# Grouped instance norm: the stores move to SP's queue, the loads to ScalarE's

## The chip, the cores and the metric

One Trainium2 chip; the program runs on one core. The time is the device time of one execution in microseconds, the median of several runs. A profile is one more execution, recorded by the hardware profiler. The engines of a core run side by side, each through its own queue of instructions in order: TensorE (PE), VectorE (DVE), ScalarE (ACT), GpSimd (POOL) and SyncE (SP). A transfer between memory and the on-chip buffer (a DMA) is issued by an instruction in the queue of SP, ScalarE or GpSimd and then carried out by the core's 16 DMA engines. An instruction waits at the head of its queue until the semaphores that it names have been raised, and all that stands behind it waits too.

## The reference

Each of 512 channels (4 images, 8 groups, 16 channels each) of 256 x 256 float32 values is normalized by its own mean and variance and scaled by its gamma:

```python
mu = x.mean(axis=(3, 4), keepdims=True)
var = ((x - mu) ** 2).mean(axis=(3, 4), keepdims=True)
x_norm = (x - mu) / np.sqrt(var + 1e-5)
out = x_norm * gamma[None, :, :, None, None]
```

Input and output have 134.22 MB each.

## The kernel before

A channel's 65,536 values are laid over S = 8 partitions, 8,192 to a partition, so 16 channels fill the 128 partitions. Such a piece is a unit: 128 x 8192 float32, 4,194,304 bytes, 32 KB to a partition. There are U = 32 units, and one loop over u (line 105) handles them. Six slots in the on-chip buffer (`slots`, AHEAD = 6) hold units: unit u lies in slot u % 6 from its load to the landing of its store, and is normalized in place. In the profile the slots appear as `xt`.

Ahead of the loop, GpSimd issues a small store into the output (`touch`, line 54, 16 x 128 values) and the load of gamma (line 55). The loads of units 0 to 5 are issued at line 57: units 1 and 3 by ScalarE, units 0, 2, 4 and 5 by SP. A loop of 60 `nop` calls for VectorE follows (lines 59 and 60). Then come constants: `navg`, a 128 x 128 matrix that adds up the 8 partitions of a channel and divides by minus the count; a first square root on ScalarE (line 78), which brings the table load with it; gamma spread over the partitions by VectorE and eight small matmuls (lines 83 to 94).

For a unit, in this order:

- line 107, VectorE: the sum over each partition, into `st`. It waits for the unit's load.
- line 108, ScalarE: the square with the sum of squares, into `st`. It waits for the same load. Its elementwise result goes to `junk`.
- line 116, TensorE: matmul of `navg` with `st`. It gives every partition minus the mean and minus the mean square (`ps`).
- line 117, VectorE: minus the variance (`nvar`).
- line 121, ScalarE: the standard deviation (`std`), called the root below.
- lines 125 and 127, VectorE: its reciprocal, times gamma (`scale`).
- line 130, VectorE: (value minus mean) times scale, in place in the slot.
- line 134, ScalarE's queue: the store of the unit, which waits for line 130.
- line 136, SP's queue: the load of unit u + 6 (through `load`, line 48), which waits until store u has landed, since it writes into the same slot.

The order is the program's own (`manual_schedule`): within an engine's queue the instructions stand as the loop writes them. So ScalarE's queue holds, for each unit, square, root, store; SP's queue holds loads alone; a load that waits on SP holds up only later loads, and a store that waits on ScalarE holds up the next unit's square.

Of the kernel before, what the change touches and what calls it, by code (L numbers as in the profile page):

```python
# [1 line left out]

# [4 lines left out]

F32 = mybir.dt.float32
U8 = mybir.dt.uint8
ALU = mybir.AluOpType  # L10
ACTF = mybir.ActivationFunctionType
AX = mybir.AxisListType


@with_exitstack
def kernel(
    ctx: ExitStack,
    tc: tile.TileContext,
    x: bass.AP,
    gamma: bass.AP,  # L20
    out: bass.AP,
):
    nc = tc.nc
    B, G, C, H, W = x.shape
    P = nc.NUM_PARTITIONS
    HW = H * W
    n_ch = B * G * C
    S = 8
    K = P // S
    F = HW // S  # L30
    U = n_ch // K
    NG = (G * C) // K
    AHEAD = 6
    assert HW % S == 0 and (G * C) % K == 0

    xv = x.rearrange("b g c h w -> (b g c h w)").rearrange("(u p f) -> u p f", p=P, f=F)
    ov = out.rearrange("b g c h w -> (b g c h w)").rearrange("(u p f) -> u p f", p=P, f=F)
    gv = gamma.rearrange("g c -> (g c)")

    data = ctx.enter_context(tc.tile_pool(name="data", bufs=1))  # L40
    singles = ctx.enter_context(tc.tile_pool(name="singles", bufs=1))
    psum = ctx.enter_context(tc.tile_pool(name="psum", bufs=4, space=bass.MemoryType.PSUM))
    ctx.enter_context(tc.manual_schedule())

    slots = [data.tile([P, F], F32, name=f"xt{i}") for i in range(AHEAD)]

    def load(u, queue):
        queue.dma_start(out=slots[u % AHEAD][:], in_=xv[u])  # L48


    g_row = singles.tile([1, G * C], F32, name="g_row")
    touch = singles.tile([16, 128], F32, name="touch")
    nc.vector.memset(touch[:], 0.0)  # L53
    nc.gpsimd.dma_start(out=ov[0][0::S, 0:128], in_=touch[:])  # L54
    nc.gpsimd.dma_start(out=g_row[:], in_=gv[None, :])  # L55
    for u in range(AHEAD):
        load(u, nc.scalar if u in (1, 3) else nc.sync)

    for _ in range(60):
        nc.vector.nop()  # L60

    eps_t = singles.tile([P, 1], F32, name="eps_t")
    nc.gpsimd.memset(eps_t[:], 1e-5)
    one = singles.tile([1, 1], F32, name="one")
    nc.gpsimd.memset(one[:], 1.0)
    navg = singles.tile([P, K, S], F32, name="navg")
    nc.gpsimd.memset(navg[:], -1.0 / HW)  # L67
    nc.gpsimd.affine_select(  # L68
        out=navg[:], in_=navg[:], pattern=[[-S, K], [0, S]], compare_op=ALU.is_ge,
        fill=0.0, base=0, channel_multiplier=1,  # L70
    )
    nc.gpsimd.affine_select(  # L72
        out=navg[:], in_=navg[:], pattern=[[S, K], [0, S]], compare_op=ALU.is_ge,
        fill=0.0, base=S - 1, channel_multiplier=-1,
    )
    navg_w = navg[:].rearrange("p k s -> p (k s)")
    root_eps = singles.tile([P, 1], F32, name="root_eps")
    nc.scalar.activation(out=root_eps[:], in_=eps_t[:], func=ACTF.Sqrt)  # L78
    g_rep = singles.tile([1, NG, K, S], F32, name="g_rep")
    g_ps = psum.tile([P, NG], F32, name="g_ps", bufs=1)  # L80
    g_col = singles.tile([P, NG], F32, name="g_col")

    nc.vector.tensor_copy(  # L83
        out=g_rep[:],
        in_=g_row[:].rearrange("o (n k) -> o n k", n=NG).unsqueeze(3).to_broadcast([1, NG, K, S]),
    )
    for n in range(NG):
        nc.tensor.matmul(  # L88
            out=g_ps[:, n : n + 1],
            lhsT=g_rep[:, n].rearrange("o k s -> o (k s)"),  # L90
            rhs=one[:],
            start=True, stop=True,
        )
    nc.vector.tensor_copy(out=g_col[:], in_=g_ps[:])  # L94

    junk = singles.tile([P, F], U8, name="junk")

    st = singles.tile([P, U, 2], F32, name="st")
    nvar = singles.tile([P, U], F32, name="nvar")
    std = singles.tile([P, U], F32, name="std")  # L100
    rstd = singles.tile([P, U], F32, name="rstd")
    scale = singles.tile([P, U], F32, name="scale")

    squares = []
    for u in range(U):
        t = slots[u % AHEAD]
        nc.vector.reduce_sum(out=st[:, u, 0:1], in_=t[:], axis=AX.X)  # L107
        square = nc.scalar.activation(  # L108
            out=junk[:], in_=t[:], func=ACTF.Square, accum_out=st[:, u, 1:2],
        )  # L110
        if u:

            tc.declare_no_dep(square.ins, squares[-1].ins, reason="junk, ordered by the root between")
        squares.append(square)
        ps = psum.tile([P, 2], F32, name="ps")
        nc.tensor.matmul(out=ps[:], lhsT=navg_w, rhs=st[:, u], start=True, stop=True)  # L116
        nc.vector.tensor_scalar(  # L117
            out=nvar[:, u : u + 1], in0=ps[:, 0:1], scalar1=ps[:, 0:1],
            scalar2=ps[:, 1:2], op0=ALU.mult, op1=ALU.add,
        )  # L120
        nc.scalar.activation(  # L121
            out=std[:, u : u + 1], in_=nvar[:, u : u + 1], func=ACTF.Sqrt,
            bias=eps_t[:], scale=-1.0,
        )
        nc.vector.reciprocal(out=rstd[:, u : u + 1], in_=std[:, u : u + 1])  # L125
        g = u % NG
        nc.vector.tensor_mul(  # L127
            out=scale[:, u : u + 1], in0=rstd[:, u : u + 1], in1=g_col[:, g : g + 1],
        )
        nc.vector.tensor_scalar(  # L130
            out=t[:], in0=t[:], scalar1=ps[:, 0:1], scalar2=scale[:, u : u + 1],
            op0=ALU.add, op1=ALU.mult,
        )
        nc.scalar.dma_start(out=ov[u], in_=t[:])
        if u + AHEAD < U:
            load(u + AHEAD, nc.sync)


# [1 line left out]
_INS = ['x', 'gamma']  # L140
_OUTS = [((4, 8, 16, 256, 256), 'float32')]


# [23 lines left out]
```

## Time and profile before

| | |
|---|---|
| median of 3 runs | 627.01 us (626.89 to 627.01) |
| span of the profiled execution | 625.8 us |
| moved | 268.46 MB, mean 429 GB/s over the span |
| VectorE busy | 443.4 us (71%) |
| ScalarE busy | 238.8 us (38%) |
| TensorE busy | 21.4 us (3%) |
| line 107, reduction | 32 x 8684 ns |
| line 108, square | 32 x 7030 ns |
| line 130, normalize | 32 x 4550 ns |
| store, issue to landing | 62.5 us (median) |
| load by SP, issue to landing | 38.5 us (median) |

The profile has several views. The page's slices cut the span into 40 equal parts and give the busy share of each engine in tenths and what the DMA engines moved. The table by stretch gives the same for chosen intervals; its columns are the interval, its length, the busy time of each engine with the number of instructions, the granted clock, the DMA share and GB/s (a packet counts where it starts). The timeline lists instructions by their start, with the engine's idle time ahead of them and what ended it in brackets; a letter q behind an engine's name means its queue, where DMAs are issued. The chain of waits follows the work that ended last backwards from step to step. The DMA queues of the hardware have numbers: q1, q10, q0 (GpSimd's) and q14 (the fetching of instructions). The trace also records every DMA packet with its queue, start, duration and size; a data packet here has 32 KB.

### The profile page before, as it was taken

What the parts mean: (1) busy time and instruction counts of PE and PEld (TensorE: products, weight loads), DVE (VectorE), ACT (ScalarE), POOL (GpSimd) and SP (SyncE); (2) the same over time, 40 slices, a digit from 0 to 9 for tenths busy, and PEclk for the clock granted to TensorE, in tenths of its full rate; (3) what the DMA queues carried; (4) which work ended last, traced back from release to release, by engine and by line L of the source; (5) the groups of instructions that cost most, each with busy time, mean ns of one, the idle gap of its engine ahead of it and who ended that gap; (6) DMA issues with size and microseconds to landing.
All of it is one profiled execution on the core that took longest, in us unless ns stands there. A gap on an engine that the chain in (4) does not pass through costs nothing.

```text
span 625.8 us, 631 instructions
## 1 busy us (share of the span) xinstructions
PE 21.4 (3%) x80; PEld 19.5 (3%) x80; DVE 443.4 (71%) x163; ACT 238.8 (38%) x98; POOL 2.4 (0%) x11
## 2 busy tenths in 40 slices
PE   0200000000000000000000000000000000000000
PEld 0200000000000000000000000000000000000000
DVE  0588999999776687766776667867668676686730
ACT  0444444444443244432344423444224442244400
POOL 1000000000000000000000000000000000000000
DMA  8999999999999999999999999999999999999998
GB/s 369 436 415 429 429 436 436 436 436 434 424 434 434 434 436 434 431 429 434 436 436 436 436 431 427 431 436 431 436 434 434 429 434 436 436 436 436 429 425 354
DMA packets 9282, 268.46 MB, mean 429 GB/s; under 512 B 1072, under 2 KB 1088, under 8 KB 1088
## 3 DMA queue, kind: packets, MB, share of 16 engines
q10 hardware_dynamic: 4896, 142.61, 52.9%
q1 hardware_dynamic: 4320, 125.83, 46.7%
q0 software_dynamic: 64, 0.01, 0.0%
q14 instruction: 2, 0.02, 0.0%
HBM read 134.22 MB, written 134.23 MB: 429 GB/s over the span
## 4 chain that ended last, share of the span: by engine, by line
another core or an unknown queue 61%; DMA 17%; DVE 15%; SPq 1%; PE 1%; issue 0%; ACT 0%
DVE st L107 10%; DMA xt<-in_x_dram 10%; DMA out_dram<-xt 8%; DVE xt L130 5%; SPq L48 1%; PE ps L116 1%; ACT std L121 0%; DVE nvar L117 0%; DVE rstd L125 0%; DVE scale L127 0%
## 5 line engine op out<-in xcount | busy, mean ns | idle before, releaser
L107 DVE TENSOR_REDUCE st<-xt 128x1 f32<-128x8192 f32 x32 | 277.9, 8684 | 101.2 <-DMA xt<-in_x_dram 101.2
L108 ACT ACTIVATE junk<-xt 128x8192 uint8<-128x8192 f32 x32 | 225.0, 7030 | 276.0 <-DMA xt<-in_x_dram 232.8
L130 DVE TENSOR_SCALAR xt<-xt,ps,scale 128x8192 f32<-128x8192 f32 x32 | 145.6, 4550 | 1.2
L121 ACT ACTIVATE std<-nvar,eps_t 128x1 f32<-128x1 f32 x32 | 9.4, 294 | 79.6 <-DVE nvar L117 79.6
L116 PE MATMUL ps<-st,navg 128*128 128x2 f32 x64 | 17.9, 349 | 558.0 <-DVE st L107 558.0
L116 PEld LDWEIGHTS ps<-st,navg 128*128 128x128 f32 x64 | 16.0, 311 | 559.8 <-issue 559.8
L117 DVE TENSOR_SCALAR nvar<-ps 128x1 f32<-128x1 f32 x32 | 9.2, 287 | 23.8 <-PE ps L116 23.8
L125 DVE RECIPROCAL rstd<-std 128x1 f32<-128x1 f32 x32 | 5.2, 164 | 11.6 <-ACT std L121 11.6
L83 DVE COPY g_rep<-g_row 1x1024 f32<-1x1024 f32 x1 | 0.7, 680 | 14.3 <-DMA g_row<-in_gamma_dram 14.3
L108 ACT ACTIVATION_READ_ACCUMULATOR junk<-xt 128x1 f32 x32 | 6.0, 187 | 0.0
L127 DVE TENSOR_TENSOR scale<-rstd,g_col 128x1 f32<-128x1 f32 x32 | 5.1, 159 | 1.1
L88 PE MATMUL g_ps<-one,g_rep 1*128 1x1 f32 x16 | 3.5, 346 | 16.2 <-DVE g_rep L83 16.2
L88 PEld LDWEIGHTS g_ps<-one,g_rep 1*128 1x128 f32 x16 | 3.5, 325 | 16.1 <-issue 16.1
L94 DVE COPY g_col<-g_ps 128x8 f32<-128x8 f32 x1 | 0.2, 166 | 3.7 <-PE g_ps L88 3.7
L78 ACT ACT_TABLE_LOAD x1 | 1.3, 1283 | 1.7 <-PEq L151 1.7
L53 DVE MEMSET touch<- 16x128 f32 x1 | 0.2, 165 | 0.9 <-PEq L151 0.9
L54 POOL DMA_DIRECT2D out_dram<-touch x1 | 0.6, 619 | 0.8 <-DVE touch L53 0.8
L55 POOL DMA_DIRECT2D g_row<-in_gamma_dram x1 | 0.5, 487 | 0.0
L68 POOL TENSOR_SCALAR_AFFINE_SELECT navg<-navg 128x128 f32<-128x128 f32 x1 | 0.4, 400 | 0.1
L72 POOL TENSOR_SCALAR_AFFINE_SELECT navg<-navg 128x128 f32<-128x128 f32 x1 | 0.4, 399 | 0.1
L67 POOL MEMSET navg<- 128x128 f32 x1 | 0.2, 232 | 0.0
L78 ACT ACTIVATE root_eps<-eps_t 128x1 f32<-128x1 f32 x1 | 0.2, 202 | 0.0
(6 smaller groups left out, 0.6 us busy)
## 6 DMA issues: line engine op xcount, KB each, us to landing
out_dram<-xt ACTq DMA_DIRECT2D x32, 4096.0 KB, 62.5
xt<-in_x_dram SPq DMA_DIRECT2D x30, 4096.0 KB, 38.5
xt<-in_x_dram ACTq DMA_DIRECT2D x2, 4096.0 KB, 31.6
out_dram<-touch POOLq DMA_DIRECT2D x1, 8.0 KB, 9.1
g_row<-in_gamma_dram POOLq DMA_DIRECT2D x1, 0.5 KB, 13.3
```

The lines of the kernel that those rows point to most:

```text
L48: queue.dma_start(out=slots[u % AHEAD][:], in_=xv[u])
L78: nc.scalar.activation(out=root_eps[:], in_=eps_t[:], func=ACTF.Sqrt)
L83: nc.vector.tensor_copy(out=g_rep[:], in_=g_row[:].rearrange("o (n k) -> o n k", n=NG).unsqueeze(3).to_broadcast([1, NG, K, S]),)
L88: nc.tensor.matmul(out=g_ps[:, n : n + 1], lhsT=g_rep[:, n].rearrange("o k s -> o (k s)"), rhs=one[:], start=True, stop=True,)
L107: nc.vector.reduce_sum(out=st[:, u, 0:1], in_=t[:], axis=AX.X)
L108: square = nc.scalar.activation(out=junk[:], in_=t[:], func=ACTF.Square, accum_out=st[:, u, 1:2],)
L116: nc.tensor.matmul(out=ps[:], lhsT=navg_w, rhs=st[:, u], start=True, stop=True)
L117: nc.vector.tensor_scalar(out=nvar[:, u : u + 1], in0=ps[:, 0:1], scalar1=ps[:, 0:1], scalar2=ps[:, 1:2], op0=ALU.mult, op1=ALU.add,)
L121: nc.scalar.activation(out=std[:, u : u + 1], in_=nvar[:, u : u + 1], func=ACTF.Sqrt, bias=eps_t[:], scale=-1.0,)
L125: nc.vector.reciprocal(out=rstd[:, u : u + 1], in_=std[:, u : u + 1])
L127: nc.vector.tensor_mul(out=scale[:, u : u + 1], in0=rstd[:, u : u + 1], in1=g_col[:, g : g + 1],)
L130: nc.vector.tensor_scalar(out=t[:], in0=t[:], scalar1=ps[:, 0:1], scalar2=scale[:, u : u + 1], op0=ALU.add, op1=ALU.mult,)
```

## The change

Three edits. The loads of units 1 and 3 are issued by SP, those of units 0, 2, 4 and 5 by ScalarE. All stores are issued by SP, so they stand in its queue behind its two loads. The loads from unit 6 on are issued by ScalarE, and not at the end of unit u for unit u + 6 but at the end of unit u for unit u + 3 (u - BEHIND + AHEAD with BEHIND = 3): in ScalarE's queue the load of unit u + 3 stands behind the root of unit u and ahead of the square of unit u + 1. It still waits for the landing of the store that frees its slot, store u - 3. The 60 `nop` calls go.

```diff
     AHEAD = 6
+    BEHIND = 3
...
     for u in range(AHEAD):
-        load(u, nc.scalar if u in (1, 3) else nc.sync)
-
-    for _ in range(60):
-        nc.vector.nop()
+        load(u, nc.sync if u in (1, 3) else nc.scalar)
...
-        nc.scalar.dma_start(out=ov[u], in_=t[:])
-        if u + AHEAD < U:
-            load(u + AHEAD, nc.sync)
+        nc.sync.dma_start(out=ov[u], in_=t[:])
+
+        if BEHIND <= u and u - BEHIND + AHEAD < U:
+            load(u - BEHIND + AHEAD, nc.scalar)
```

In the program as built, ScalarE's queue then holds four loads, the table load and the first root; square and root of units 0 to 3; load 6; square and root of unit 4; load 7; and so on to load 31 behind root 28. SP's queue holds loads 1 and 3 and the 32 stores. 29 waits that stood as instructions of their own at line 134 in ScalarE's queue are gone from it. VectorE's queue has the same 165 rows in both programs, and no `nop` among them in either.

## The prediction

> **What bounds the kernel now.** I read the page's slices first, then the DMA queues, then the stretches, then the chain of waits and the timeline around one steady unit.
>
> ```profile
> span 625.8 us, 631 instructions
> ...
> DMA  8999999999999999999999999999999999999998
> ...
> q10 hardware_dynamic: 4896, 142.61, 52.9%
> q1 hardware_dynamic: 4320, 125.83, 46.7%
> ...
> q14 instruction: 2, 0.02, 0.0%
> ```
>
> The 16 DMA engines are full in every slice but the first and the last. q10 carries 34 transfers of 4,194,304 bytes (142.61 MB: the 32 stores and two loads, so it is ScalarE's queue); q1 carries the 30 loads that SP issues.
>
> ```profile
> 0.00:1.80 1.80, 0.00 (x0) 0.00 (x0) 0.17 (x1) 0.08 (x1) 0.64 (x5) 1.00 0.00 0
> ...
> 39.00:43.00 4.00, 0.00 (x0) 0.00 (x0) 4.00 (x1) 4.00 (x1) 0.00 (x0) 1.00 0.96 328
> ...
> 200.00:500.00 300.00, 8.92 (x32) 8.01 (x32) 216.19 (x80) 117.65 (x48) 0.00 (x0) 1.00 1.00 433
> ...
> 622.80:623.70 0.90, 0.00 (x0) 0.00 (x0) 0.00 (x0) 0.00 (x0) 0.00 (x0) 1.00 0.09 36
> ```
>
> The last two columns are DMA share and GB/s. For 300 us in the middle the share is 1.00 at 433 GB/s, while DVE is busy 216 of 300 us. So the time is a sum of bytes: 268.46 MB at 433 GB/s = 620.0 us. Add 1.80 us before the first packet: 621.8. The other 4.0 us of the span are, by the same table, about 1.0 us in the stretch 39 to 43 (4 x (1 - 328/433)), 0.45 us in the first packets (1.80 to 15.60 ran at 419 GB/s: 13.8 x (1 - 419/433)), and the end. There 36 GB/s over 0.9 us is 32 KB, one packet: in the records of the single packets 15 engines finish between 622.86 and 623.65 us and one at 624.49, and 1.3 us follow up to the span's end. The median of the runs is 627.01, 1.2 us above the span; I keep that 1.2.
>
> So a change can gain only the ragged edges, and it can lose only by leaving DMA engines without a packet.
>
> ```profile
> 543.09 0.34 ACTq L134 DMA_DIRECT2D out_dram<-xt  x1
> 547.40 7.03 ACT L108 ACTIVATE junk<-xt 128x8192 uint8<-128x8192 f32 x1 [9.32 <-DMA xt<-in_x_dram]
> 547.40 8.69 DVE L107 TENSOR_REDUCE st<-xt 128x1 f32<-128x8192 f32 x1 [4.34 <-DMA xt<-in_x_dram]
> 547.61 0.33 SPq L48 DMA_DIRECT2D xt<-in_x_dram  x1
> ```
>
> This is steady state, one unit every 19.36 us. Unit 29's load lands at 547.40 and starts square and reduction; store 25 lands and lets SP issue load 31 at 547.61.
>
> ```profile
> out_dram<-xt ACTq DMA_DIRECT2D x32, 4096.0 KB, 62.5
> xt<-in_x_dram SPq DMA_DIRECT2D x30, 4096.0 KB, 38.5
> ```
>
> A store takes 62.5 us from issue to landing, 3.2 periods; a load 38.5, two periods. So about three stores and two loads are queued at any time. These queues are the cover for everything below.
>
> **The change, part by part.**
>
> *The nops.* The order of VectorE's instructions is the same before and after, 165 rows, and holds no nop: the loop emits nothing. 0 us. If nops did run, they would fall into VectorE's 14.27 us of waiting for gamma ahead of the copy at line 83, and the first reduction waits until 22.62 for its load anyway.
>
> *The first loads.* ScalarE issues four (0, 2, 4, 5) in place of two (1, 3). Four took SP 1.92 us, two took ScalarE 0.88, so the table load starts 1.04 us later, at 2.8, and the first root on line 78 ends near 4.3. ScalarE is not needed before 22.62. Both queues issue their first load at 0.81 as before and share the engines equally. 0 us.
>
> *The stores on SP.* 32 issues of 0.34 us move off ScalarE. SP does nothing else but two loads, so store u goes out when VectorE's line 130 is done, as before. In units 0 to 7 ScalarE's square no longer waits behind the store (5.4 us eight times, 43.2 in all), but VectorE sets that pace: 14.93 us a unit (22.62 to 37.56), reduction 8.69 against square 7.03 + 0.19. 0 us.
>
> *Loads from unit 6 on.* Load u+3 stands behind root u on ScalarE and waits for store u-3. Issue times before were 62.39, 81.71, 101.08, 120.44 and 139.82 for loads 6 to 10. The roots ahead of them now, those of units 3 to 7, stand in the chain of waits (start, duration):
>
> ```profile
> 77.17 0.30 ACT std L121
> ...
> 92.10 0.30 ACT std L121
> ...
> 107.03 0.30 ACT std L121
> ```
>
> and, on the timeline, 121.97 and 136.90. They end 0.3 us later. Lateness: 77.5 - 62.4 = 15.1 us, then 10.8, 6.3, 1.9, and none for load 10, where the store's landing comes last again. Does load 6's lateness empty the load queue? Load 5 took 79.3 us from its issue at 2.16, so it lands near 81.5. From issue to first packet it is 1.0 us (0.81 to 1.80) to 2.3 us (store 0, 37.67 to 39.93), so load 6 starts between 78.5 and 79.8: in time by 1.7 to 3.0 us. If it did miss, stores 1 and 2 (issued at 52.61 and 67.54) would keep all engines busy. VectorE comes to unit 6 at 112.22 and load 6 still lands near 101. 0 us.
>
> *The wait in ScalarE's queue.* Behind the waiting load stand square u+1, root u+1, and through them VectorE's line 117, the apply and store u+1. By the timeline above the store's landing comes 0.2 us after the load's, and the issue takes 0.34: the square starts at about 547.97, 0.57 us late, and ends at 555.2, while the reduction that the same matmul needs ends at 556.09. Hidden by 0.9 us. Were the store one packet later (1.2 us, 32 KB at a sixteenth of 433 GB/s), the unit would be 0.3 us late, with 62.5 - 19.4 = 43 us of stores queued ahead of it. 0 us.
>
> *The end.* From the chain of waits:
>
> ```profile
> 547.61 38.49 DMA xt<-in_x_dram
> ...
> 596.59 4.55 DVE xt L130
> ```
>
> Load 31 is still released by store 25 near 547.6 and lands at 586.1; its line 130 ends at 601.1, and store 31 is issued at 601.2. Its first packet could go at 603.5 (2.3 later), while the stores ahead last until 624.5 - 9.7 = 614.8 (4.19 MB at 433 GB/s). Slack 11.3 us. 0 us.
>
> *The instruction queue.* q14 moved two packets of 8 KB inside the span; the packet records put them at 156.5 and 199.3 us, 0.31 us each. The first lies on the very engine that finishes last, and the data packet behind it took 0.53 us more than the usual 1.21. Without the two that engine would end 0.84 us earlier, level with the next one (623.65). The change leaves ScalarE a shorter program (29 waits by themselves at line 134 go), so this fetch may vanish, move or stay. No row says which: bounds -0.84 and +0.84 (the same on another late engine). I take -0.2, near to nothing, because the other engines' programs keep their length or nearly so. The Trainium skill, "Runtime: NRT & Kernel Launch", section "Instruction fetch mechanics", says that crossing a fetch boundary is mostly hidden; by it the term is 0 and the sum 627.0. The row shows a fetch in the path of the engine that ends last, so the trace agrees only in part.
>
> Sum: 625.8 - 0.2 = 625.6 in the profile, + 1.2 = 626.8 us.
>
> **The rivals.**
>
> *A, the ragged end closes.* Which engine ends last is decided by a few slow packets. If every engine ended like the earliest, 622.86, the span would lose 1.63 us: 625.4. For it: the latest engine is alone. Against it: six or more engines end at 623.5 or later through slow packets near 2 and 41 us, when first loads and first stores start, and those starts stay; that leaves 0.84, or 626.2.
>
> *B, slower: ScalarE's lateness lasts.* If load 6's 15.1 us are not made good, because each late load makes its store and so the load six units on late, load 31 lands at 601.2 and its store is issued at 616.3. It decides from 11.3 us of lateness on; beyond that the engines run dry: 15.1 - 11.3 = 3.8 us, 630.8. For it: the loads now sit in the queue of an engine that also computes. Against it: the lateness shrinks by 4.4 us a unit, since roots come every 14.93 us and stores land every 19.36, and is gone at load 10. The Trainium skill, "DMA: Bandwidth & Descriptors", section "Anatomy of one DMA", says that a semaphore wait is held by the issuing sequencer and not by the DMA engines; by that rule square and root do stand behind the load. The trace agrees: in units 0 to 7 the square waits for the line 130 that releases the store ahead of it, 5.4 us each.
>
> *C, slow packets elsewhere.* Exchanging the two rings may bring further stretches like 39 to 43, at 0.8 to 1.0 us each; two of them give 628.6. For it: that stretch exists and the page does not explain it. Against it: 300 us at a constant 433 GB/s, and the same pairs of load and store still run side by side.
>
> **How the numbers follow.** Forecast 0.70, A 0.12, B 0.10, C 0.08. The range goes from 625.8 (most of A left out) to 628.2 (a packet of 1.2 us more on the last engine); B and the far ends of A and C stay outside. I count 0.2% (1.25 us) as what a measurement of this kernel can tell from no change. Faster 0.07 (A's larger part), slower 0.13 (B and part of C), within 0.80.
>
> **What would show it.** Right: 433 GB/s and a DMA share of 1.00 from 60 to 580 us; q1 and q10 with their counts exchanged except for the first loads (q1 34 transfers, q10 30); loads 6 to 9 issued near 77.5, 92.4, 107.4 and 122.3, then one each 19.4 us; squares up to a microsecond behind their reductions; store 31 issued near 601 with the engines busy to 624. Wrong: a slice in the middle under 420 GB/s, reductions ending before their squares, or engines dry between the last load and the last store.

## The result, and the profile after

| | before | changed |
|---|---|---|
| median | 626.91 us (20 runs) | 629.83 us (20 runs) |
| lowest and highest | 626.75 to 627.49 | 626.73 to 649.27 |
| ratio | | 1.0047 (95% interval 1.0030 to 1.0064) |
| span of the profiled execution | 625.8 | 626.8 |
| that execution's own time | not on record | 628.55 |

Here and below a ratio leaves out executions more than 1.5% above the fastest of their kernel, here the one of 649.27; the granted clock was 1.00 in all of them. The change made the kernel slower by half a percent, and the interval is clear of 1. The striking part is the scatter: the kernel before repeats within 0.8 us, the changed one takes anything from 626.7, the time of before, to 635, and once 649. Its profiled execution is one of the faster ones, so the first trace shows the effect only in small.

From the page of the changed kernel, slices and queues:

```profile
span 626.8 us, 607 instructions
...
DMA  8999999999999999999999999999999999999997
...
q1 hardware_dynamic: 4896, 142.61, 52.8%
q10 hardware_dynamic: 4320, 125.83, 46.6%
...
out_dram<-xt SPq DMA_DIRECT2D x32, 4096.0 KB, 62.5
xt<-in_x_dram ACTq DMA_DIRECT2D x30, 4096.0 KB, 38.5
```

The two queues have exchanged their counts, and a store still takes 62.5 us and a load 38.5 from issue to landing: the same three stores and two loads are queued. The DMA engines are as full as before. The steady state on the timeline is the forecast one too:

```profile
548.43 8.69 DVE L105 TENSOR_REDUCE st<-xt 128x1 f32<-128x8192 f32 x1 [4.35 <-DMA xt<-in_x_dram]
548.60 0.33 ACTq L49 DMA_DIRECT2D xt<-in_x_dram  x1
548.98 7.03 ACT L106 ACTIVATE junk<-xt 128x8192 uint8<-128x8192 f32 x1 [9.88 <-DMA out_dram<-xt]
```

Unit 29's square starts 0.55 us behind its reduction, because the load in front of it on ScalarE waited for a store. It ends at 556.0 us, the reduction at 557.1. This wait costs nothing. The difference shows in the table by stretch (interval, length, busy times, clock, DMA share, GB/s):

```profile
39.00:43.00 4.00, 0.00 (x0) 0.00 (x0) 4.00 (x1) 0.88 (x2) 0.00 (x0) 1.00 0.92 311
...
90.00:113.00 23.00, 1.12 (x4) 1.00 (x4) 20.65 (x11) 13.09 (x5) 0.00 (x0) 1.00 1.00 430
...
200.00:500.00 300.00, 8.93 (x32) 8.02 (x32) 216.54 (x77) 118.38 (x47) 0.00 (x0) 1.00 1.00 433
...
624.20:625.60 1.40, 0.00 (x0) 0.00 (x0) 0.00 (x0) 0.00 (x0) 0.00 (x0) 1.00 0.05 23
```

39 to 43 lost more than before (311 GB/s against 328), 90 to 113 ran 1% low, and at the end one packet of 32 KB (23 GB/s over 1.4 us) is still to be moved when the other engines have finished. In the packet records 15 engines end between 622.82 and 624.00 us and one at 625.52. That one lost 2.1 us in eight consecutive store packets between 92 and 111 us; its load packets in between kept their 1.21 us.

The packet records do not name the engine. But an engine's packets follow each other without a gap, so 16 chains can be followed by time; the numbers 0 to 15 below are the order of their first packets. A ring here is one hardware queue's waiting line of packets at an engine. Each engine takes packets from the two queues' rings in turn: in the kernel before no engine takes two packets of one ring in a row between 38 and 580 us. By the timelines the first store is issued at almost the same time in both kernels:

```profile
37.67 0.35 ACTq L134 DMA_DIRECT2D out_dram<-xt  x1
```

```profile
37.87 0.35 SPq L132 DMA_DIRECT2D out_dram<-xt  x1
```

The first is the kernel before, the second the changed one. This is how three chains go on when loads 2 and 3 end (start in us; an extra duration of a packet over 1.21 us in parentheses):

```
before,  0:  38.83 load 2   40.04 load 3 (+0.30)   41.57 load 4 (+0.46)   43.24 store 0
changed, 3:  38.93 load 3   40.15 load 2 (+0.57)   41.94 store 0          43.15 load 4
changed, 8:  38.88 load 3   40.09 load 2 (+0.49)   41.80 load 4 (+0.69)   43.70 store 0
```

In the kernel before, the first turn of a round belongs to SP's ring, and ScalarE's ring with store 0 comes second: store 0 is not asked for until 43.2. In the changed kernel the stores sit in SP's ring, so store 0 is asked for at 41.7 to 42.4. Eleven engines find it there. Five (0, 1, 2, 6 and 8), whose turn came at 41.67 to 41.80, do not: they take a second load packet and write store 0 one packet later. From then on these five write while the other eleven read. Engine 8 is the one that ends last; it is the only one of the five whose store packets are late between 60 and 150 us, so being out of step does not cost every time. In the kernel before no engine misses a turn at that place. I call this the turn theory. Its rivals are that the exchanged queues themselves cost time, and that late loads do.

### The profile page after: what moved, and what is told of

Its sections match the earlier page's. It is cut to its first block, busy times and chain, and to the rows that moved or that the text cites. A ratio compares the mean times of both kernels' runs of the same rounds, so it can differ in the third digit from the quotient of the medians.

```text
span 626.8 us, 607 instructions
## 1 busy us (share of the span) xinstructions
PE 21.4 (3%) x80; PEld 19.5 (3%) x80; DVE 443.4 (71%) x163; ACT 238.5 (38%) x98; POOL 2.4 (0%) x11
## 4 chain that ended last, share of the span: by engine, by line
DMA 60%; DVE 23%; another core or an unknown queue 11%; PE 1%; ACT 1%; issue 1%
DMA xt<-in_x_dram 53%; DVE st L105 18%; DMA out_dram<-xt 7%; DVE xt L128 4%; PE ps L114 1%; ACT std L119 1%; DVE nvar L115 1%; DVE rstd L123 0%; DVE scale L125 0%
## 6 DMA issues: line engine op xcount, KB each, us to landing
out_dram<-xt SPq DMA_DIRECT2D x32, 4096.0 KB, 62.5
xt<-in_x_dram ACTq DMA_DIRECT2D x30, 4096.0 KB, 38.5
```

## The experiments

All kernels were timed beside the kernel before on the same chip; its median was 626.87 to 626.97 in every group.

**The changed kernel again** (no edit).

> The changed kernel itself, once more, for a second trace and a second sample of its times. All theories: times scattered from 627 to 635 us around 629 to 630, the kernel before at 627.0 within 0.5. The trace should show the middle of the kernel at 433 GB/s and one DMA engine that ends 1 to 8 us behind the others; in the first trace that engine lost 2.1 us in eight store packets between 92 and 111 us.

Measured: 629.95 us median, 627.01 to 639.76 in 12 runs; ratio 1.0050 (1.0024 to 1.0075). The second trace is of a longer execution, span 633.9:

```profile
60.00:80.00 20.00, 1.12 (x4) 1.01 (x4) 17.64 (x10) 9.80 (x5) 0.00 (x0) 1.00 1.03 446
80.00:150.00 70.00, 2.24 (x8) 2.01 (x8) 59.00 (x22) 28.21 (x13) 0.00 (x0) 1.00 1.00 421
200.00:500.00 300.00, 8.37 (x30) 7.51 (x30) 212.95 (x77) 113.26 (x46) 0.00 (x0) 1.00 1.00 433
...
624.50:632.00 7.50, 0.00 (x0) 0.00 (x0) 0.00 (x0) 0.00 (x0) 0.00 (x0) 1.00 0.18 79
```

The loss lies between 80 and 150 us (421 GB/s), and at the end a DMA share of 0.18 means that three engines of 16 work on alone. Seven engines missed the turn near 41 us; four of them missed another near 81 us, which put them back in step. The three that were left out of step have all the slow packets worth naming between 80 and 150 us, and all three end at 632.6, nine microseconds behind the median engine.

**Late loads alone.** SP keeps the loads and ScalarE the stores, with the lateness of the changed kernel:

```diff
...
-        if u + AHEAD < U:
-            load(u + AHEAD, nc.sync)
+        if BEHIND <= u and u - BEHIND + AHEAD < U:
+            late = load(u - BEHIND + AHEAD, nc.sync)
+            tc.add_manual_dep(late.ins, root.ins.name, ...)
```

> The kernel before with one part of the change alone: SP still issues the loads and ScalarE the stores, but the load of unit u+3 also waits for the root of unit u, so loads 6 to 9 are as late as in the changed kernel (15, 11, 6 and 2 us). Theory late loads (a load queue with one transfer less between 62 and 140 us lets a DMA engine fall behind): scattered as the changed kernel, median 629 to 630. Theory exchanged queues (stores in SP's ring or loads issued by ScalarE): 627.0 within 0.5, no scatter.

Measured: 630.14 us median, 627.55 to 675.98 in 10 runs; ratio 1.0041 (1.0023 to 1.0060). The queues are those of the kernel before, and it scatters more than the changed kernel: exchanged queues are not needed for the loss. By the expectation this spoke for late loads. But its trace (span 674.3) shows where it starts. From the page:

```profile
GB/s 376 434 416 432 426 424 420 424 422 424 426 428 426 424 420 428 408 432 418 430 414 420 402 414 404 412 410 422 391 424 412 393 420 402 424 406 330 272 218 101
```

At 16.9 us a slice, the rate drops from the fifth slice on and comes back only for single slices. Near 41 us no engine missed a turn. Near 81 us load 6 was asked for:

```
gate,  0:  79.52 store 1   80.74 store 2           82.02 load 6   83.23 store 2
gate, 15:  79.98 store 1   81.20 load 6            82.41 store 2  83.62 load 6
```

Load 6 was issued at 77.42:

```profile
77.42 0.33 SPq L49 DMA_DIRECT2D xt<-in_x_dram  x1
```

Fourteen engines, with turns at 80.7 to 81.1, did not find it; two (11 and 15), with turns at 81.17 and 81.20, did. Those two are now the ones out of step, and from 84 to 151 us each of their 22 store packets took 0.62 us more than the usual 1.21, while their loads took nothing more. These two also end last, at 672.6 and 672.9, the others by 660.4. So it is not missing a turn that costs: here those pay that are in the minority.

**The first loads alone.** Line 57 of the kernel before with `nc.sync if u in (1, 3) else nc.scalar`.

> The kernel before with another part alone: the first six loads change queues (1 and 3 on SP, 0, 2, 4 and 5 on ScalarE), all later loads stay on SP and all stores on ScalarE. Store 0 now stands behind loads 4 and 5 in ScalarE's ring. Theory first loads (the order of the two rings in the first 60 us): scattered, 629 to 630. Theories late loads and exchanged queues: 627 within 0.7, no scatter.

Measured: 627.04 us median, 626.93 to 627.23 in 11 runs; ratio 1.0001 (0.9992 to 1.0009). No scatter. Store 0 stands behind two loads in its ring, so all 16 engines take load packets one after the other alike. Later in its trace (span 625.3) all 16 engines take two packets of one ring in a row at each transfer's end, because loads and stores no longer end in the same round; that costs nothing here.

**No late load.** The changed kernel with `BEHIND = 2`.

> The changed kernel with BEHIND = 2: load u+4 stands behind root u and waits for store u-2, so load 6 goes out near 62.4 as in the kernel before and no load is late; ScalarE waits longer (the square of unit 6 starts near 121), and one store less is queued. Queues as in the changed kernel. Theory late loads: 627.0 to 627.5, no scatter. Theory exchanged queues: scattered as the changed kernel, 629 to 630.

Measured: 628.49 us median, 626.69 to 634.36 in 11 runs; ratio 1.0028 (1.0007 to 1.0049). It scatters though load 6 goes out at 62.5, so late loads are not needed either. Both expectations in their plain form had failed: each single part can do it alone. In the trace two engines (1 and 13) missed the turn for store 0, at 42.27, and these two end at 625.49 and 625.40 while the other 14 have ended by 623.79. Nine of the 14 had found store 0 at turns a little earlier, 42.09 to 42.20; the table below comes back to this.

**Store 0 later, first attempt.** A square over 1440 or 2160 elements ahead of store 0 in ScalarE's queue:

```diff
+        if u == 0:
+            nc.scalar.activation(out=junk[:, 0:1440], in_=t[:, 0:1440], func=ACTF.Square)
         nc.scalar.dma_start(out=ov[u], in_=t[:])
```

> The kernel before with only store 0 issued 1.4 us later (a square over 1440 elements of the normalized unit 0, result unused, stands ahead of it in ScalarE's queue: 37.67 becomes 39.1). Turn theory: each DMA engine takes a packet from the two rings in turn; where the next transfer of a ring is not ready at an engine's turn, the engine takes a second packet of the other ring and stays one packet out of step with the engines that found it ready; the few that are out of step then have slow store packets, and the last engine ends the kernel. Store 0 is ready some 4.2 us after its issue (41.9 in the changed kernel), and in the kernel before its turn comes at 43.2 to 43.5. 1.4 us later it is ready at about 43.3, so some engines find it and some do not: scattered, 627 to 635. Rival exchanged queues: 627.0 within 0.5, since the queues are those of the kernel before.

> The same with 2160 elements, 2.0 us later (about 39.7), so that store 0 is ready near 43.9, between two turns. Turn theory: all 16 engines miss the turn alike, stay in step, and the time is 627.0 within 0.5, without scatter, though the store is later than in the kernel with 1.4 us. Rival late transfer (the later a transfer, the worse, whichever engines it hits): scattered as with 1.4 us or more.

Measured: 626.90 (626.71 to 627.53) and 627.04 (626.78 to 627.64), 11 runs each; ratios 1.0000 (0.9991 to 1.0008) and 1.0002 (0.9993 to 1.0010). These tell nothing about the theory, for the store was not held up. The trace of the first:

```profile
37.64 1.40 ACT L135 ACTIVATE junk<-xt 128x1440 uint8<-128x1440 f32 x1 [5.08 <-DVE xt L130]
37.66 0.35 ACTq L136 DMA_DIRECT2D out_dram<-xt  x1
```

The store is issued 0.02 us after the square began, not after it ended.

**The other ring first.** SP's first load (load 0 in the kernel before, load 1 in the changed kernel with `BEHIND = 2`) waits for the memset of `touch`:

```diff
...
+        if u == 0:
+            tc.add_manual_dep(ld.ins, first.ins.name, ...)
...
```

> The kernel before with one wait: SP's first load waits for the memset of line 53 and goes out at about 1.1 instead of 0.81, so ScalarE's ring (which carries the stores) takes the first turn. Turn theory: store 0's turn comes one packet earlier, near 41.7, across the time at which it is ready, as in the changed kernel: scattered, 627 to 635. Rival exchanged queues: 627.0 within 0.5 (plus 0.3 at most for the later first load).

> The changed kernel with BEHIND = 2 (load 6 goes out near 62.4) and SP's first load behind the memset, so that ScalarE's ring takes the first turn and SP's ring, which carries the stores, the second. Queues and issuing engines stay exchanged. Turn theory: store 0's turn comes near 43.2, after it is ready, load 6 is early: all engines in step, 627.0 within 0.5, no scatter. Rival exchanged queues: scattered as before this edit, 628 to 630.

Measured: the kernel before with this wait, 633.62 us median, 629.31 to 652.72 in 7 runs, ratio 1.0072 (1.0044 to 1.0099). SP's first load goes out 0.27 us later (1.08 for 0.81), and through it store 0 goes out at 39.02 instead of 37.67. In the trace (span 628.2) 13 engines found store 0 and three did not; the three end last, at 625.3 to 626.9, the others by 623.9. That is enough for the loss without exchanged queues, and it speaks for the turns. The second, 643.45 us, 642.36 to 644.32 in 4 runs, ratio 1.0260 (1.0247 to 1.0274): the mending failed. The trace says why it was no clean test. The wait let ScalarE's ring have two packets before SP's first, so loads 0 and 1 no longer end in the same round. From there all 16 engines take two packets of one ring in a row at each transfer's end; in the first of the two kernels only the three that missed store 0 do. In such double turns a transfer is passed over even where it was issued early: store 0, issued at 36.83, at 42.6 to 43.2 by all 16. It is another state than the one that I meant to make. Why this kernel is slow stays open: with the first loads alone all 16 engines take such double turns too, at 627.04.

**Store 0 later, held in fact.** As the first attempt, on the kernel before, and the store waits for the end of the square.

> The kernel before with store 0 alone made later: it waits for the end of a square over 1440 elements (result unused), so it goes out near 39.1 instead of 37.67. (The two earlier kernels of this kind did not hold it up, their store still went out at 37.7 and 37.8.) Turn theory: store 0 becomes ready some 4.2 us after its issue, near 43.3, across its turn at 43.2 to 43.5, so that some DMA engines find it and others do not: scattered, 627 to 635, and the engines out of step with the rest end last. Rival exchanged queues: 627.0 within 0.5, since the queues are those of the kernel before.

> The same with 2160 elements, store 0 near 39.8 and ready near 44.0, between two turns. Turn theory: all engines miss the turn alike and stay in step: 627.0 within 0.7, no scatter; if its trace shows that only some engines missed the turn, scattered. Rival late transfer (the later the worse): slower and more scattered than with 1440 elements. Rival exchanged queues: 627.0.

Measured with 1440 elements: 661.58 us median, 634.31 to 674.98 in 6 runs (too scattered for a ratio). From its timeline:

```profile
39.27 0.35 ACTq L136 DMA_DIRECT2D out_dram<-xt  x1
```

A store that goes out 1.6 us later, one of 32 and not on the way to any other work at that time, makes the kernel 7 to 48 us longer. Thirteen engines missed its turn (42.7 to 43.1), three found it (43.40 to 43.65). In this trace (span 669.5) the three end last, at 665.3 to 668.2, the others by 655.6. With 2160 elements it went out at 39.82: 643.46 us median, 642.13 to 644.05 in 5 runs, ratio 1.0260 (1.0247 to 1.0273). My forecast of 627 for that one failed. All engines missed the first turn, but seven missed a second one, so they did not stay in step; from there all 16 take double turns at each transfer's end, as in the other kernel of 643 us. It also falsifies the rival "the later the worse".

**Store 0 earlier.** The changed kernel, with ScalarE normalizing 2048 columns of unit 0 beside VectorE's 6144:

```diff
...
+        n = F
+        if u == 0:
+            n = 6144
+            nb = singles.tile([P, 1], F32, name="nb")
+            nc.vector.tensor_mul(out=nb[:], in0=ps[:, 0:1], in1=scale[:, 0:1])
+            nc.scalar.activation(out=t[:, n:F], in_=t[:, n:F], func=ACTF.Identity, bias=nb[:], scale=scale[:, 0:1])
...
```

> The changed kernel with BEHIND = 2 (load 6 out near 62.5) and store 0 about 1 us earlier, near 36.8: for unit 0 alone ScalarE normalizes the last 2048 columns while VectorE does 6144. Queues stay exchanged and SP's ring still takes the first turn. Turn theory: store 0 is ready near 41.0, ahead of its turn at 41.6 to 42.3 on all engines; nobody is out of step: 627.0 within 0.7, no scatter (BEHIND = 2 without this: 626.7 to 634.4). Rival exchanged queues: scattered, median 628 to 630.

> The same early store 0 with the changed kernel's BEHIND = 3, so load 6 goes out near 77.5 again, for a turn near 81. Turn theory: only the second place is left at which engines can miss a turn (in the second trace of the changed kernel and in the kernel with the gated loads some did at 80.7 to 81.1): scattered as there, median 628 to 630. Late loads harmless: 627.0 within 0.7.

Measured: 626.90 us with `BEHIND = 2` (626.67 to 628.53, 11 runs; ratio 1.0000, 0.9991 to 1.0008) and 626.80 with `BEHIND = 3` (626.65 to 628.64, 11 runs; ratio 1.0003, 0.9994 to 1.0012). The scatter is all but gone with the queues still exchanged: one execution of 22 at 627.79 and three at 628.5 to 628.64 remain. From the trace of the first, the store and two stretches:

```profile
36.92 0.34 SPq L140 DMA_DIRECT2D out_dram<-xt  x1
```

```profile
60.00:150.00 90.00, 3.45 (x12) 3.02 (x12) 70.91 (x30) 37.38 (x16) 0.00 (x0) 1.00 1.01 434
200.00:500.00 300.00, 9.39 (x32) 8.01 (x32) 210.35 (x80) 117.27 (x48) 0.00 (x0) 1.00 1.00 433
```

No engine missed a turn, and all 16 end between 622.94 and 623.75. With `BEHIND = 3` one engine missed the turn for store 0 (issued at 37.14); that execution took 628.64, the longest of the eleven. The expectation for it was half wrong: load 6 went out at 76.64 and nobody missed its turn near 81.

**Control for the early store.** The same split with `BEHIND = 3`, and store 0 held back to its old time by a square over 840 elements that it waits for.

> Control for the early store: the same kernel (BEHIND = 3, unit 0 normalized by VectorE and ScalarE together), but store 0 waits for a square over 840 elements and goes out near 38.0 again, where the changed kernel has it (37.87). Turn theory: scattered again, 627 to 640, with some engines out of step from 41 to 42 us on. If the split of the work were what helped: 626.8, no scatter.

Measured: 629.69 us median, 626.76 to 640.61 in 12 runs; ratio 1.0037 (1.0013 to 1.0062). The scatter is back, so it was the moment and not the split. From its timeline and its table by stretch (span 636.8):

```profile
37.74 0.34 SPq L142 DMA_DIRECT2D out_dram<-xt  x1
```

```profile
60.00:150.00 90.00, 3.35 (x12) 3.01 (x12) 74.33 (x30) 37.27 (x16) 0.00 (x0) 1.00 1.01 429
...
200.00:500.00 300.00, 8.36 (x30) 7.51 (x30) 212.59 (x78) 111.46 (x46) 0.00 (x0) 1.00 1.00 433
...
624.50:635.00 10.50, 0.00 (x0) 0.00 (x0) 0.00 (x0) 0.00 (x0) 0.00 (x0) 1.00 0.12 53
```

This is the cleanest picture. For the last 10.5 us two engines of 16 work alone (0.12; 53 GB/s is twice 27). Two engines, 5 and 14, missed the turn for store 0, and they are the two that end at 635.48 and 635.12; the other 14 have ended by 623.67. Between 60 and 150 us their store packets took 0.34 to 0.35 us more on average, their load packets nothing, and engine 0's neither.

**Load 6 a little earlier.** The kernel with gated loads, waiting for the reduction in place of the root.

```diff
-                late.ins, root.ins.name,
+                late.ins, total.ins.name,
```

> The kernel with gated loads, but the load of unit u+3 waits for the reduction of unit u instead of its root: load 6 goes out near 76.2 instead of 77.4, still 14 us later than in the kernel before. Turn theory, with about 4 us from issue to ready: ready near 80.2, ahead of its turn at 80.7 to 81.2 on all engines: 627.0 within 0.7, no scatter. Theory late loads: scattered as with the root, 627.5 to 676.

Measured: 627.25 us median, 626.67 to 627.61 in 11 runs; ratio 1.0002 (0.9993 to 1.0011).

```profile
76.23 0.33 SPq L49 DMA_DIRECT2D xt<-in_x_dram  x1
```

Load 6 at 76.23 in place of 77.42, still 13.8 us later than in the kernel before: no engine misses a turn, no scatter. Late loads as such cost nothing.

In one table, by the first trace of each kernel; "missed" counts the engines that did not find the new transfer at the turn named:

| kernel | issued | missed | times (us) |
|---|---|---|---|
| before | store 0 at 37.67, second turn | 0 of 16 | 626.75 to 627.49 |
| changed | store 0 at 37.87, first turn | 5 | 626.73 to 649.27 |
| changed, BEHIND 2 | store 0 at 37.87, first turn | 2 | 626.69 to 634.36 |
| early store, BEHIND 2 | store 0 at 36.92, first turn | 0 | 626.67 to 628.53 |
| early store held back | store 0 at 37.74, first turn | 2 | 626.76 to 640.61 |
| before, store 0 held (1440) | store 0 at 39.27, second turn | 13 | 634.31 to 674.98 |
| gated loads, root | load 6 at 77.42, first turn | 14 | 627.55 to 675.98 |
| gated loads, reduction | load 6 at 76.23, first turn | 0 | 626.67 to 627.61 |

The moment of the turn does not sort the engines in every trace. In the second trace of the changed kernel turns up to 42.11 were missed while others found store 0 from 41.92 on; with `BEHIND = 2` the two missed turns (42.26 and 42.28) come later than nine that were found. What sorts them better is when the packet ahead of the turn started:

| trace | issued | missed, latest start | found, earliest start |
|---|---|---|---|
| changed, first | 37.87 | 40.09 | 40.15 |
| changed, second | 37.92 | 40.12 | 40.18 |
| changed, BEHIND 2 | 37.87 | 39.92 | 40.36 |
| before, store 0 held (1440) | 39.27 | 41.61 | 41.65 |
| gated loads, root | 77.42 | 79.92 | 79.96 |

In four more traces (early store with `BEHIND = 3`, its control, SP's first load waiting on the kernel before, store 0 held with 2160 elements) some engines fall on the wrong side of any such line. So the time of issue decides how many engines miss, but what an engine looks at, and when, stays open.

## Why the prediction was wrong

The bound was right: 16 full DMA engines and a sum of bytes, 433 GB/s in the middle of both kernels. So were most terms of the sum. ScalarE's wait ahead of the square is hidden (0.55 us late, as against 0.57 forecast), loads 6 to 8 go out when forecast (77.37 for load 6), and the drain at the end has no hole. Rival B, lasting lateness on ScalarE, did not happen: the steady state is back by load 10. The instruction fetch stayed: two packets again, and what lies around the span was 1.75 us in the profiled execution, not the 1.2 that I kept. In every run with both figures on record it is 1.66 to 1.78; the 1.2 set the median of some runs against the span of another execution, and with 1.7 the same sum gives 627.3.

**The step that failed** is "The stores on SP", costed at 0 us "as before", together with "Both queues issue their first load at 0.81 as before and share the engines equally". The change cost 2.9 us at the median. Equal shares are not equal turns. SP's ring has the first turn of a round, and moving the stores there moved store 0's turn from 43.2 to near 41.7 us. Store 0, issued at 37.87, was not found at 41.80 and was found at 41.94. I never compared the time at which a moved transfer is ready with the time at which its ring is asked.

**Two sentences made that possible.** The first took 1.0 to 2.3 us from issue to first packet, from an idle start (0.81 to 1.80) and from a store whose packet I had misread: the one at 39.93 belongs to load 3. What the runs show on busy engines is longer: load 6 was taken 3.8 us after its issue at the earliest (81.18 after 77.42), store 0 4.0 us after (41.92 after 37.92), and single engines missed turns as late as 5.2 us (42.94 after 37.74) and 6.1 us (43.21 after 37.14, early store with `BEHIND = 3`). So the margin of 1.7 to 3.0 us that I gave load 6 was none. The second was "If it did miss, stores 1 and 2 (...) would keep all engines busy", hence 0 us. They do keep them busy. But an engine that has missed a turn alone, or found it alone, writes while the others read, and where it paid, its stores took 0.3 to 0.6 us a packet more over many packets; the kernel ends with the slowest engine.

Rival C came nearest: it named slow packets after an exchange of the rings and 628.6, at a chance of 0.08. It had no place and no condition for them. Its objection, that the same pairs of load and store run side by side, holds for one engine and overlooks the step between engines. The range was built on one packet more on the last engine; the scatter is of many packets.

Shown by the experiments: the moment at which one transfer is issued decides, in both directions, whichever queue carries it (early store and its control; gated loads by root and by reduction). Read from the traces: where one to three engines are out of step, these are the ones that end last. Only argued: that reading neighbours are what slows the writer. Left open: through which resource, why four of the five out of step in the first trace of the changed kernel lost nothing between 60 and 150 us, why the loss of an engine stops after some 70 us in some executions (the second trace of the changed kernel is at 433 GB/s from 200 us on) and runs to the end in others, and how many engines must be out of step to be safe as a majority.

## What to carry to other kernels

Where two queues keep the DMA engines full, a transfer has to be issued well before its ring is asked for it. Here all 16 engines found a transfer that was issued 4.5 us (gated loads by the reduction) or 5.1 us (early store with `BEHIND = 2`) ahead of the first turn; 3.3 to 4.2 us split them, and at 4.9 us (early store with `BEHIND = 3`) one engine still missed. A transfer already queued behind another is the safe form in the kernel before, whose steady state shows no missed turn. A median alone would have called this change half a percent; the spread of the runs (0.8 us against 8 and more) was the first sign that something is decided by chance within a microsecond. When engines work in parallel on parts of every transfer, look at which one ends last and at what moment it left the others.

## What the runs showed of the hardware that I had not expected

- From issue to the first packet of a transfer: 1.0 us on idle engines, 3.8 us at the earliest on busy ones whose ring has just run out (load 6, 81.18 after 77.42), and one engine passed over a transfer at 6.1 us.
- 16 DMA engines that alternate between a read and a write ring keep step for 580 us (kernel before: no missed turn on any engine up to there, 12 store and load packets over 0.1 us late after 60 us). Two engines out of step paid 0.62 us on each of 22 store packets in a row (1.83 for 1.21 us) and nothing on their loads. In the first trace of the changed kernel four of five paid nothing.
- Where transfers of the two rings no longer end in the same round, an engine takes double turns at each transfer's end, and that goes on through the kernel. Two kernels in which all 16 engines do so took 643.45 and 643.46 us, 16.5 us more than the kernel before; a third (first loads alone) took 627.04, so the double turns alone do not set the price.
- A DMA in ScalarE's queue does not wait for the computation ahead of it: it was issued 0.02 us after a square of 1.40 us had begun.
